# Hybrid attention and retention block: ScalarE issues the stores of its own results, retention is gated where it is computed, the states of both heads are built first, and the output projection takes its rows in order of readiness

## The chip, the cores and the metric

One core of one Trainium2 chip. Its engines run side by side, each through its own queue in order: TensorE (PE in the profile; PEld is its weight load), VectorE (DVE), ScalarE (ACT), GpSimd (POOL) and SyncE (SP, which computes nothing and issues transfers between HBM and the on-chip memory). The metric is the device time of one execution in microseconds; lower is better.

## What is computed

One encoder block on a sequence of 1024 tokens, model width 2048, all in float32. Cut to what matters:

```
h    = rmsnorm(x, norm_w)
q_a, k_a, v_a, g_a, q_r, k_r, v_r, g_r = split(h @ w_in)          # 2048 x 5632
attn = windowed_attention(q_a, k_a, v_a)    # 16 heads, 4 key/value heads, +-128 tokens
attn = rmsnorm(attn, w1) * silu(g_a)                              # width 1024
ret  = bidirectional_retention(rotary(q_r), rotary(k_r), v_r)     # 8 heads, chunks of 128
ret  = head_groupnorm(ret, w2) * silu(g_r)                        # width 1024
out  = rmsnorm(x + concat([attn, ret]) @ w_out, final_norm_w)     # 2048 x 2048
```

Retention runs over chunks in both directions: within a chunk it is a masked product, across chunks a state per head is carried, `state = state * decay + k^T v`.

## The kernel before

Each float32 operand of a large product is split into a high part (`wh`, `hT` part 0, rounded by ScalarE) and a low part (`wl`, the rest, by a subtraction on VectorE or GpSimd), and three matmuls (high x high, high x low, low x high) replace one. The program runs in four stretches:

- **The standard units** (`STD`, lines 1161 to 1163): keys, values and queries of the attention, 6 units.
- **The first half of the fast units** (`FAST`, 16 units of 256 columns: `ga` and `gr` are the gates, `qk` the retention's queries and keys, `vr` its values). A unit is a 2x2 block product done with 7 passes in place of 8, 12 matmuls each (`multiply`, lines 981 to 983), first over one half of the contraction, whose partial results go to HBM (`yd`), then over the other half. `prep` splits the weights of a pass two passes (slots) ahead, on ScalarE and GpSimd; `collect` adds a finished PSUM bank to the unit's result tile `e`, on VectorE. Attention (`attn_job`, 4 groups) is woven into this half.
- **The second half of the fast units**. A finished tile goes through `deliver`: gates through a SiLU on ScalarE and to HBM (`gd`, line 1059 and the store after it), values through a transpose on TensorE (`to_tokens`, lines 1086 and 1088), queries and keys through the rotary step (`rope`). Retention (`ret_job(p)`, 4 pairs p of 2 heads) is woven in here, and `premix`, which multiplies the attention's rows by their gates and norms on GpSimd.
- **The output projection** (lines 1295 to 1297, then 1321 to 1323): 16 rows k of `w_out` for each of 7 units `un`, 12 matmuls a row; `mixed_load` and `mixed_rows` bring the mixed activations of a row (`kk`, 0 to 7 attention, 8 to 15 retention) into `hT`.

What is woven in is cut into steps by `yield`. `point()` is called after every three matmuls, and every `pace` points it emits one step of `jobs` (attention, retention) and every `apace` points one of `aux` (premix and the like). So the text that a queue holds is written by the recording order; a scheduler that orders each engine's instructions then moves some past each other. `store()` does not issue at once: it keeps a store for some points (`delay`, 7 by default) and then gives it to SP. `lag(n, f)` runs `f` n slots later.

Of a pair p of retention the steps are: `k_tr` (transpose the keys), `s_t` (masked scores), `kv(ah, h)` (products of keys and values of head ah, sequence half h, and on VectorE the state tile `ST`, lines 707, 709 and 153), `o_mm` (output: lines 736 and 738, the second of which reads `ST`; statistics on VectorE), `o_fin`, `o_norm` (normalisation, line 766, ScalarE), `o_tr` (transpose, lines 773 and 776, store). One buffer `ST` serves both heads, so `kv(1, .)` stands after the outputs of head 0.

Buffers that matter: `t2` (6 tiles for everything in passing), `r` (9, weights of fast units), `e11`, `e12` (2 each), `e21`, `e22` (1 each, results of a unit and weights to come).

## Time and profile before

| | |
|---|---|
| time, 3 runs | 1571.16, 1574.75 (median), 1576.69 us |
| the profiled execution | 1579.63 us; its span in the trace 1577.9 us |
| TensorE, VectorE, ScalarE, GpSimd busy | 1485.4 (94%), 896.2, 675.1, 639.3 us |
| mean granted TensorE clock | 0.978 |
| HBM traffic | 216.38 MB read, 93.88 MB written |

The busy time of TensorE includes matmuls that wait in its pipeline and those that run at the lower clock, so the losses are read from its waits and from the granted clock, stretch by stretch. All 1145 transfers of the program are issued by SP.

### The profile page before, as it was taken

What the parts mean: (1) busy time and instruction counts of PE and PEld (TensorE: products, weight loads), DVE (VectorE), ACT (ScalarE), POOL (GpSimd) and SP (SyncE); (2) the same over time, 40 slices, a digit from 0 to 9 for tenths busy, and PEclk for the clock granted to TensorE, in tenths of its full rate; (3) what the DMA queues carried; (4) which work ended last, traced back from release to release, by engine and by line L of the source; (5) the groups of instructions that cost most, each with busy time, mean ns of one, the idle gap of its engine ahead of it and who ended that gap; (6) DMA issues with size and microseconds to landing.
All of it is one profiled execution on the core that took longest, in us unless ns stands there. A gap on an engine that the chain in (4) does not pass through costs nothing. (4 is left out here: it accounts for less than half of the span.)

```text
span 1577.9 us, 22010 instructions
## 1 busy us (share of the span) xinstructions
PE 1485.4 (94%) x7250; PEld 1233.9 (78%) x7250; DVE 896.2 (57%) x1856; ACT 675.1 (43%) x1417; POOL 639.3 (41%) x497
## 2 busy tenths in 40 slices
PE   8999999999999999999988988998879979999997
PEld 6898877878888888887867866777658767888886
DVE  6565346854664664668756767667485423364323
ACT  5311135865765775776322332433434423334210
POOL 3232221346556547555775565555641010113000
PEclk9999999999999999999999999999998999999999
DMA  8878768884454465538785675566855644566403
GB/s 302 290 263 304 265 177 266 263 251 156 154 159 146 149 182 174 153 112 289 240 281 182 194 235 176 189 181 196 269 170 160 235 146 158 156 215 207 125 27 107
DMA packets 195406, 311.73 MB, mean 198 GB/s; under 512 B 29355, under 2 KB 67243, under 8 KB 194652
## 3 DMA queue, kind: packets, MB, share of 16 engines
q1 hardware_dynamic: 195292, 310.33, 61.1%
q8 instruction: 57, 0.93, 0.3%
q14 instruction: 57, 0.47, 0.1%
HBM read 216.38 MB, written 93.88 MB: 197 GB/s over the span
## 5 line engine op out<-in xcount | busy, mean ns | idle before, releaser
L150 POOL TENSOR_TENSOR wl<-r,wh 128x512 fp32r<-128x512 f32 x224 | 302.4, 1356 | 287.9 <-ACT wh L156 278.3
L981 PE MATMUL psMa<-hT,wh 128*128 128x512 f32 x512 | 209.9, 410 | 4.4 <-DVE e L150 3.9
L156 ACT CAST wh<-r 128x512 fp32r<-128x512 f32 x224 | 137.5, 617 | 174.4 <-PE psMa L982 81.7
L983 PE MATMUL psMa<-hT,wl 128*128 128x512 f32 x512 | 203.5, 397 | 2.0 <-POOL wl L150 2.0
L982 PE MATMUL psMa<-hT,wh 128*128 128x512 f32 x512 | 203.0, 396 | 0.0
L156 ACT CAST wh<-e 128x512 fp32r<-128x512 f32 x160 | 97.6, 618 | 208.6 <-PE psMb L1297 74.3
L981 PE MATMUL psMb<-hT,wh 128*128 128x512 f32 x384 | 156.5, 408 | 4.3 <-DVE bnt L153 4.3
L983 PE MATMUL psMb<-hT,wl 128*128 128x512 f32 x384 | 152.9, 398 | 6.1 <-POOL wl L150 6.0
L150 DVE TENSOR_TENSOR wl<-e,wh 128x512 fp32r<-128x512 f32 x112 | 83.7, 757 | 131.8 <-ACT wh L156 126.8
L150 POOL TENSOR_TENSOR wl<-e,wh 128x512 fp32r<-128x512 f32 x48 | 71.8, 1499 | 205.0 <-ACT wh L156 197.7
L982 PE MATMUL psMb<-hT,wh 128*128 128x512 f32 x384 | 151.9, 396 | 0.0
L150 POOL TENSOR_TENSOR t<-t,t 128x512 f32<-128x512 f32 x48 | 64.5, 1345 | 134.1 <-DMA t<-gd 102.3
L983 PEld LDWEIGHTS psMa<-hT,wl 128*128 128x128 f32 x512 | 98.0, 191 | 25.6 <-POOL wl L150 3.7
L981 PEld LDWEIGHTS psMa<-hT,wh 128*128 128x128 f32 x512 | 98.4, 192 | 22.4 <-issue 4.7
L982 PEld LDWEIGHTS psMa<-hT,wh 128*128 128x128 f32 x512 | 98.5, 192 | 16.1
L590 DVE CUSTOM_DVE_ANT_0 P<-psST,bias,nsink 128x384 f32<-128x384 f32 (+1 forms) x128 | 74.3, 580 | 38.9 <-PE psST L582 37.9
L983 PEld LDWEIGHTS psMb<-hT,wl 128*128 128x128 f32 x384 | 73.2, 191 | 24.9 <-POOL wl L150 8.7
L150 DVE TENSOR_TENSOR r<-r,r 128x512 f32<-128x512 f32 x64 | 61.8, 977 | 51.2 <-POOL wl L150 50.8
L594 ACT ACTIVATE P<-P,nmx 128x385 f32<-128x385 f32 (+1 forms) x128 | 75.8, 592 | 30.8 <-DVE nmx L590 30.0
L981 PEld LDWEIGHTS psMb<-hT,wh 128*128 128x128 f32 x384 | 73.5, 191 | 17.7 <-issue 4.9
L150 POOL TENSOR_TENSOR r<-r,r 128x512 f32<-128x512 f32 x64 | 84.6, 1332 | 3.8
L982 PEld LDWEIGHTS psMb<-hT,wh 128*128 128x128 f32 x384 | 73.3, 191 | 12.4
(338 smaller groups left out, 3564.4 us busy)
## 6 DMA issues: line engine op xcount, KB each, us to landing
r<-in_w_fast SPq DMA_DIRECT2D x128, 256.0 KB, 3.4
e<-in_w_out SPq DMA_DIRECT2D x112, 256.0 KB, 3.3
yd<-e SPq DMA_DIRECT2D x64, 256.0 KB, 2.7
e<-yd SPq DMA_DIRECT2D x64, 256.0 KB, 3.2
t<-in_xT SPq DMA_DIRECT2D x31, 512.0 KB, 6.2
t<-cd SPq DMA_DIRECT2D x56, 256.0 KB, 4.0
e<-in_w_in SPq DMA_DIRECT2D x48, 256.0 KB, 5.0
md<-t SPq DMA_DIRECT2D x48, 256.0 KB, 3.1
```

Of the source, the lines that this page charges most:

```text
L150: eng.tensor_tensor(o, x, y, op)
L156: A.copy(o_hi, x)
L590: V.tensor_tensor_reduce(x[:, :W], p[:, :W], bias[2 * pr + c][:, k0 : k0 + W], -1.0, nsink[:, head : head + 1], ALU.add, ALU.min, nmx[:, c ...
L594: A.activation(x[:, : W + 1], x[:, : W + 1], AF.Exp, bias=nmx[:, c : c + 1], scale=-1.0, accum_out=sums[:, c : c + 1])
L981: T.matmul(bank, wh[:, ws], hh, start=(j == 0 and p in (0, 1, 3)), stop=False, skip_group_check=True)
L982: T.matmul(bank, wh[:, ws], hl, start=False, stop=False, skip_group_check=True)
L983: T.matmul(bank, wl[:, ws], hh, start=False, stop=(j == 3), skip_group_check=True)
```

## The change: what it does

1. `store_now`: the stores of `u` (attention outputs, 64), of the gates (32) and of `vr` (16) are issued by ScalarE right behind the operation that made them, not later by SP.
2. The order of the fast units: `gr` of a pair directly behind its `qk` and `vr`; the last two gates of the attention (`ga` 2 and 3) come last. `gate` runs 2 slots after the tile is done (before 1), `to_tokens` 3 (before 2).
3. `o_norm` loads the gate of its tile, and `o_tr` multiplies by it on VectorE while it reads the transposed result from PSUM (before: a copy on ScalarE, and the gate multiplied in later on GpSimd by `mixed_rows`).
4. Two state tiles, `ST0` and `ST1`: `kv` of both heads comes ahead of the first output; the buffer for this is that of one of the two `kT`. A pair has 34 steps for 31, at a pace of 2.42 points for 2.75.
5. Output rows are taken in the order `ROWS`, with the rows that are ready last at the end; `mixed_rows` works in three stages, one per call (wait, ScalarE, VectorE). `premix` is split by half, and half of it moves into the output projection.
6. Buffers: `e2` with 3 tiles in place of `e21` and `e22`, 8 `r` for 9; raw weights are loaded in another order; `pace` of the attention 2.65 for 2.7.

```diff
-FAST = [("ga", 0), ("qk", 0), ("vr", 0), ("qk", 1), ("vr", 1), ("ga", 1), ("qk", 2), ("vr", 2)]
-FAST += [("qk", 3), ("vr", 3), ("ga", 2), ("ga", 3)] + [("gr", _p) for _p in range(4)]
+FAST = [("ga", 0), ("qk", 0), ("vr", 0), ("gr", 0), ("qk", 1), ("vr", 1), ("gr", 1), ("ga", 1)]
+FAST += [("qk", 2), ("vr", 2), ("gr", 2), ("qk", 3), ("vr", 3), ("gr", 3), ("ga", 2), ("ga", 3)]
+ROWS = [0, 1, 2, 3, 8, 9, 10, 11, 12, 13, 4, 5, 14, 15, 6, 7]
...
+    def store_now(dst, src, then=None):
+        A.dma_start(dst, src)
+        if then is not None:
+            then()
...
-        return out_of(com, [128, 512], F32, tag, 2 if tag in ("e11", "e12") else 1)
+        return out_of(com, [128, 512], F32, tag, 3 if tag == "e2" else 2)
...
-                store(mpd[2 * g + pr, :, :, 128 * n : 128 * n + 128], u, u, last)
+                store_now(mpd[2 * g + pr, :, :, 128 * n : 128 * n + 128], u, last)
...
-            kT[h] = r4(f"kT{h}")
+            kT[h] = r4("kT")
...
-                ST[ah] = r4("ST")
+                ST[ah] = r4(f"ST{ah}")
...
+            e0 = RET + 128 * (2 * p + ah)
+            so = t2()
+            SP.dma_start(so, gd[e0 : e0 + 128, 512 * h : 512 * h + 512])
+            O[ah, h] = (on, so)
...
-            so = t2()
-            A.copy(so, q)
+            tt(V, so, q, so, ALU.mult)
...
+            ((kv, 0, 0),),
+            ((kv, 1, 0),),
             ((k_tr, 1),),
-            ((kv, 0, 0),),
             ((s_t, 0, 1),),
             ((kv, 0, 1),),
+            ((kv, 1, 1),),
             (),
             (),
             ((o_mm, 0, 0, 0),),
...
-        if kk >= 8:
-            g = t2()
-            SP.dma_start(g, gd[128 * kk : 128 * kk + 128, sl])
-        mixing.append([kk, hf, r, g])
+        if not mixed_ready(kk, hf):
+            drain(aux if kk < 8 else jobs, ("pre", kk, hf) if kk < 8 else ("ret", (kk - 8) // 2))
...
-                store(gd[128 * c : 128 * c + 128, sl], t, t, finished, 4)
-            lag(1, gate)
+                store_now(gd[128 * c : 128 * c + 128, sl], t, finished)
+            lag(2, gate)
...
-                store(dst, o.rearrange("p (c e) -> p c e", c=4), o, finished)
-            lag(2, to_tokens)
+                store_now(dst, o.rearrange("p (c e) -> p c e", c=4), finished)
+            lag(3, to_tokens)
...
-            pace[0], apace[0] = 2.75, 2.3
+            pace[0], apace[0] = 2.42, 2.2
...
-            if stage == 0:
-                drain(aux, ("pre", 7))
...
+            mixed_rows()
+            for kk in {0: (0, 1), 1: (2, 3), 3: (8, 9), 4: (10, 11), 5: (12,), 6: (13,)}.get(stage, ()):
                 mixed_load(kk, 0)
-                mixed_rows(2)
...
-                if un == 0 and k == 9:
-                    drain(jobs, ("ret", 3))
-                    mixed_load(14, 0)
-                    mixed_load(15, 0)
-                if un == 0 and k == 11:
-                    mixed_rows(0)
+                if un == 0:
+                    mixed_rows()
+                    if k in (5, 6, 7, 8, 9, 10):
+                        mixed_load(ROWS[k + 5], 0)
+                    if k == 13:
+                        mixed_flush()
```

What this does to the queues, first on VectorE where the state of the first pair is built. Before, for head 1 of the pair, behind the outputs of head 0 (names end in running numbers; `r` is a sum of weights, `bnt` a statistic, `e22` a tile of `collect`):

```order
L150 TENSOR_TENSOR r1951_9198<-r1920_9022,r1921_9023 128x512
L707 COPY ST1941_9125<-psST1940_9120 64x384
L153 SCALAR_TENSOR_TENSOR ST1941_9125<-ST1941_9125,cdec_97,psST1940_9120 64x128
L150 TENSOR_TENSOR bnt1950_9184<-bnv1934_9095,bny1935_9097 128x4
L150 TENSOR_TENSOR r1918_9020<-r1918_9020,r1920_9022 128x512
```

And in the change, for both heads ahead of the outputs (`ST0` is `ST01858`, `ST1` is `ST11866`):

```order
L717 COPY ST01858_8732<-psST1857_8727 64x384
L160 SCALAR_TENSOR_TENSOR ST01858_8732<-ST01858_8732,cdec_97,psST1857_8727 64x128 x4
L717 COPY ST11866_8769<-psST1865_8764 64x384
L160 SCALAR_TENSOR_TENSOR ST11866_8769<-ST11866_8769,cdec_97,psST1865_8764 64x128 x2
L157 TENSOR_TENSOR e12_1842_8664<-psMa1832_8627,e12_1842_8664 128x512
L160 SCALAR_TENSOR_TENSOR ST11866_8769<-ST11866_8769,cdec_97,psST1865_8764 64x128 x2
L157 TENSOR_TENSOR sd1872_8816<-psST1871_8811,dt1840_8652 128x512
L157 TENSOR_TENSOR e2_1852_8705<-psMa1799_8453,e2_1852_8705 128x512
L157 TENSOR_TENSOR r1860_8745<-r1860_8745,r1859_8744 128x512
L719 COPY ST01858_8732<-psST1876_8831 64x512
```

The work of head 1 has moved from between the two heads' outputs to directly behind that of head 0, and the chains of the two heads now share VectorE's queue. Next ScalarE in the attention: `u` is copied out of PSUM, and in the change its store follows (with what each waits for: `Activation` is ScalarE's own earlier result, `DMAHW` an earlier transfer). Before:

```order
L553 COPY u_1078_5323<-psO1077_5316 128x256 [waits DMAHW7_49,PE_49]
L571 CAST PTh1080_5329<-psST1079_5325 128x3x128 [waits PE_49]
L594 ACTIVATE P1085_5338,sums1084_5337<-P1085_5338,nmx1083_5336 128x385 [waits DVE_49]
L156 CAST wh1092_5387<-r980_4903 128x512 [waits PE_49,Pool_49]
L571 CAST PTh1080_5329<-psST1089_5363 128x3x128 [waits PE_49]
```

In the change:

```order
L563 COPY u_1082_5343<-psO1081_5336 128x256 [waits DMAHW7_49,PE_49]
L581 CAST PTh1084_5350<-psST1083_5346 128x3x128 [waits PE_49]
L107 DMA mpd_59<-u_1082_5343 256x1x128 [waits DMAHW5_49,Activation_49]
L163 CAST wh1091_5380<-r980_4904 128x512 [waits PE_49,Pool_49]
L604 ACTIVATE P1089_5359,sums1088_5358<-P1089_5359,nmx1087_5357 128x385 [waits DVE_49]
```

The store has come into ScalarE's queue one operation behind the copy, between two casts; it waits for the copy and for an earlier transfer. Last SP at the head of the output projection. Before, rows of retention with a gate each (lines 844 and 847), between stores of gates (line 98):

```order
L844 DMA t2_2480_11829<-md_58 128x512
L847 DMA t2_2481_11831<-gd_57 128x512
L844 DMA t2_2482_11836<-md_58 128x512
L847 DMA t2_2483_11838<-gd_57 128x512
L98 DMA md_58<-t2_2473_11781 128x512
L98 DMA gd_57<-e21_2448_11648 128x512
```

In the change:

```order
L780 DMA t2_2438_11690<-gd_57 128x512
L863 DMA t2_2440_11700<-md_58 128x512
L863 DMA t2_2441_11702<-md_58 128x512
L863 DMA t2_2450_11745<-md_58 128x512
L207 DMA e11_2486_11919<-in_w_out 128x512
L845 DMA t2_2457_11774<-md_58 128x512
L846 DMA t2_2458_11775<-gd_57 128x512
```

The rows come without a gate (line 863), the only gate there is that of `o_norm` (line 780), and the loads of `premix` (lines 845 and 846), which before were over by then, stand between the weights (line 207).

## Rows read from the trace of the kernel before

**Rows 1.** The page's first part: each engine's busy time, share of the span and instructions.

```profile
PE 1485.4 (94%) x7250; PEld 1233.9 (78%) x7250; DVE 896.2 (57%) x1856; ACT 675.1 (43%) x1417; POOL 639.3 (41%) x497
```

**Rows 2.** Busy time by stretch, in us: the attention's half, the retention's half, the start of the output projection, its rest. Columns: stretch, its length, PE, PEld, DVE, ACT, POOL, granted clock of TensorE (1 is the full one), share of the transfer engines, GB/s.

```profile
262.00:742.00 480.00, 470.58 (x2442) 399.91 (x2443) 295.56 (x755) 325.67 (x761) 258.33 (x196) 0.99 0.58 184
742.00:1222.00 480.00, 429.65 (x2100) 350.53 (x2099) 324.94 (x648) 167.30 (x317) 270.44 (x213) 0.95 0.65 208
1222.00:1350.00 128.00, 117.55 (x488) 93.32 (x487) 46.24 (x71) 41.92 (x80) 12.98 (x10) 0.96 0.54 175
1350.00:1577.90 227.90, 217.63 (x955) 178.52 (x953) 93.82 (x167) 62.25 (x125) 27.12 (x24) 0.99 0.44 141
```

**Rows 3.** What TensorE waited for in the retention's half (742 to 1222 us): us in total, times, longest.

```profile
PE psO L738 <- DVE ST L153: 26.2, 7, 7.1
PE psST L1086 <- DVE e L150: 6.3, 3, 2.9
PE psMb L983 <- POOL wl L150: 4.9, 4, 2.1
PE psMb L981 <- DVE bnt L153: 4.3, 1, 4.3
PE psMa L981 <- DVE e L150: 3.9, 2, 2.6
PE psMa L983 <- POOL wl L150: 2.0, 3, 0.9
```

**Rows 4.** The same at the start of the output projection (1222 to 1350 us).

```profile
PE psST L1295 <- ACT wh L156: 4.9, 3, 2.6
PE psMa L1295 <- ACT wh L156: 3.9, 2, 3.6
PE psST L1296 <- DVE wl L150: 1.0, 3, 0.4
```

**Rows 5.** Granted clock in two short stretches behind waits of TensorE (columns as in rows 2).

```profile
981.00:992.00 11.00, 6.49 (x22) 5.36 (x23) 7.34 (x20) 2.75 (x6) 1.59 (x2) 0.53 0.38 133
1182.00:1193.00 11.00, 9.21 (x29) 7.40 (x30) 10.55 (x21) 5.26 (x10) 3.48 (x3) 0.53 0.32 107
```

**Rows 6.** Two waits of line 981, the first matmul of a bank, in order of time (start, us, instruction, and in brackets the idle time before it).

```profile
981.18 0.66 PE L981 MATMUL psMa<-hT,wh 128*128 128x512 f32 x1 [1.38 <-DVE e L150]
...
1183.79 0.77 PE L981 MATMUL psMb<-hT,wh 128*128 128x512 f32 x1 [4.31 <-DVE bnt L153]
```

**Rows 7.** The seven waits of line 738 in order of time, written as in rows 6. They are pair 0 head 0, pair 0 head 1, and so on; the last is pair 3 head 0.

```profile
850.54 0.80 PE L738 MATMUL psO<-ST,qs 128*128 128x128 f32 x2 [5.98 <-DVE ST L153]
884.27 0.49 PE L738 MATMUL psO<-ST,qs 128*128 128x128 f32 x2 [1.04 <-DVE ST L153]
950.52 0.49 PE L738 MATMUL psO<-ST,qs 128*128 128x128 f32 x2 [1.74 <-DVE ST L153]
987.45 0.80 PE L738 MATMUL psO<-ST,qs 128*128 128x128 f32 x2 [4.33 <-DVE ST L153]
1049.44 0.49 PE L738 MATMUL psO<-ST,qs 128*128 128x128 f32 x2 [1.51 <-DVE ST L153]
1083.19 0.49 PE L738 MATMUL psO<-ST,qs 128*128 128x128 f32 x2 [4.55 <-DVE ST L153]
1151.26 0.80 PE L738 MATMUL psO<-ST,qs 128*128 128x128 f32 x2 [7.06 <-DVE ST L153]
```

**Rows 8.** VectorE at the last of these waits: the sum of weights ahead of the state chain, the chain's head, and its last piece.

```profile
1141.52 4.09 DVE L150 TENSOR_TENSOR r<-r,r 128x512 f32<-128x512 f32 x3 [6.95 <-POOL wl L150]
1145.64 0.69 DVE L709 COPY ST<-psST 64x512 f32<-64x512 f32 x1
...
1150.85 0.35 DVE L153 SCALAR_TENSOR_TENSOR ST<-ST,cdec 64x128 f32<-64x128 f32 x1
```

**Rows 9.** GpSimd shortly before: the multiplications of `premix` (`t<-t,t`), in pairs.

```profile
1126.04 2.66 POOL L150 TENSOR_TENSOR t<-t,t 128x512 f32<-128x512 f32 x2 [5.20 <-DMA t<-rbd]
...
1132.53 2.64 POOL L150 TENSOR_TENSOR t<-t,t 128x512 f32<-128x512 f32 x2 [2.59 <-DMA t<-rbd]
```

**Rows 10.** Groups of instructions by line: engine, operation, tiles, count, busy us, mean ns, idle before.

```profile
L862 ACT ACTIVATE hT<-t,ew 128x512 fp32r<-128x512 f32 x28 | 20.0, 720 | 41.7 <-POOL t L150 25.2 <-DMA t<-md 13.7 <-PE psMa L983 2.6
L150 POOL TENSOR_TENSOR t<-t,t 128x512 f32<-128x512 f32 x48 | 64.5, 1345 | 134.1 <-DMA t<-gd 102.3 <-DMA t<-rbd 28.7 <-DMA e<-yd 1.3
L150 DVE TENSOR_TENSOR e<-psMa,e 128x512 f32<-128x512 f32 x80 | 54.2, 682 | 29.4 <-PE psMa L983 26.7 <-ACT e L1018 1.7 <-issue 0.5
```

**Rows 11.** Transfers by kind: median us from issue to landing.

```profile
mpd<-u SPq DMA_DIRECT2D x64, 128.0 KB, 2.7
...
t<-gd SPq DMA_DIRECT2D x32, 256.0 KB, 4.5
```

**Rows 12.** One issue of a store on SP, in order of time (start, us it took).

```profile
1101.61 0.38 SPq L98 DMA_DIRECT2D md<-t  x1
```

**Rows 13.** What the stores of SP (line 98) waited for: us in total, times, longest.

```profile
SPq L98 <- ACT e L1059: 45.3, 20, 5.2
...
SPq L98 <- ACT u L553: 9.7, 3, 4.8
```

**Rows 14.** One matmul of 512 columns at the full clock, from the chain of work that ended last (start, us, what).

```profile
1319.23 0.23 PE psMa L1297
```

More of the change, by code (lines that the diff above doesn't have):

```diff
@@ L116, in et_ @@
     def et_(tag):
-        return out_of(com, [128, 512], F32, tag, 2 if tag in ("e11", "e12") else 1)
+        return out_of(com, [128, 512], F32, tag, 3 if tag == "e2" else 2)
     def rt(dt):
-        return wp.tile([128, 512], dt, tag="r", name=nm("r"), bufs=9)
+        return wp.tile([128, 512], dt, tag="r", name=nm("r"), bufs=8)
     def wpair(i):
@@ L191, in w_src @@
         if i >= W_STD:
-            return a["w_out"][(i - W_STD) % 64]
+            i -= W_STD
+            return a["w_out"][(ROWS[i] if i < 16 else i) % 64]
         u, j = divmod(i, 8)
@@ L519, in attn_job @@
         SP.dma_start(vs3[:, :, 64:128].bitcast(F32), vd[g])
-        yield
-        yield
+        for _ in range(4):
+            yield
+        vr3 = vs3[:, :, 64:128].bitcast(F32)
+        for hf in range(2):
+            sl = slice(512 * hf, 512 * hf + 512)
+            A.copy(kh[:, sl], kl[:, sl].bitcast(F32))
+        A.copy(vs3[:, :, 0:64], vr3)
         yield
@@ L823, in hybrid_block @@
     mixing = deque()
-    def premix(kk):
-        for hf in range(2):
-            sl = slice(512 * hf, 512 * hf + 512)
-            r, g, n = t2(), t2(), t2()
-            SP.dma_start(r, md[128 * kk : 128 * kk + 128, sl])
-            SP.dma_start(g, gd[128 * kk : 128 * kk + 128, sl])
-            SP.dma_start(n, rbd[:, sl])
-            for _ in range(3):
-                yield
-            tt(G, g, g, n, ALU.mult)
-            tt(G, r, r, g, ALU.mult)
-            yield
-            store(md[128 * kk : 128 * kk + 128, sl], r, r, (lambda: done.add(("pre", kk))) if hf else None)
-            yield
@@ L841, in mixed_load, with premix @@
-    def mixed_load(kk, hf):
-        r, g = t2(), None
-        sl = slice(512 * hf, 512 * hf + 512)
-        SP.dma_start(r, md[128 * kk : 128 * kk + 128, sl])
-        if kk >= 8:
-            g = t2()
-            SP.dma_start(g, gd[128 * kk : 128 * kk + 128, sl])
-        mixing.append([kk, hf, r, g])
-    def mixed_rows(keep):
-        for m in list(mixing)[: max(len(mixing) - 1, 0) if keep else None]:
-            if m[3] is not None:
-                tt(G, m[2], m[2], m[3], ALU.mult)
-                m[3] = None
-        while len(mixing) > keep:
+    def premix(kk, hf):
+        sl = slice(512 * hf, 512 * hf + 512)
+        r, g, n = t2(), t2(), t2()
+        SP.dma_start(r, md[128 * kk : 128 * kk + 128, sl])
+        SP.dma_start(g, gd[128 * kk : 128 * kk + 128, sl])
+        SP.dma_start(n, rbd[:, sl])
+        for _ in range(5):
+            yield
+        tt(G, g, g, n, ALU.mult)
+        tt(G, r, r, g, ALU.mult)
+        yield
+        store(md[128 * kk : 128 * kk + 128, sl], r, r, lambda: done.add(("pre", kk, hf)))
+        yield
@@ L857, in mixed_rows, with mixed_ready @@
+    def mixed_ready(kk, hf):
+        return ("pre", kk, hf) in done if kk < 8 else ("ret", (kk - 8) // 2) in done
+    def mixed_load(kk, hf):
+        if not mixed_ready(kk, hf):
+            drain(aux if kk < 8 else jobs, ("pre", kk, hf) if kk < 8 else ("ret", (kk - 8) // 2))
+        r = t2()
+        SP.dma_start(r, md[128 * kk : 128 * kk + 128, 512 * hf : 512 * hf + 512])
+        mixing.append([kk, hf, r, 0])
+    def mixed_rows():
+        while mixing and mixing[0][3] == 2:
             kk, hf, r, _ = mixing.popleft()
@@ L866, in evac, with mixed_flush @@
+    def mixed_flush():
+        while mixing:
+            mixed_rows()
     def evac(u, b, p, st):
@@ L940, in hybrid_block, with raw_room @@
     raws, sums, ready_w, banks, outs = {}, {}, {}, {}, {}
-    def raw_room(q):
+    def raw_room(q, which):
         if q < 2 * NF:
-            for x in (2, 1, 3, 0):
+            for x in which:
                 raws[q, x] = rt(F32)
@@ L1182, in hybrid_block @@
     step[0] = 16 * NS
[L1183 removed]
+    old, coming = deque(), deque()
     for n, (q, p) in enumerate(slots):
```

81 lines of the change are left out of this document (39 added, 42 removed).

## Prediction

> **What bounds the kernel now.** I read the busy shares first: TensorE is busy for 1485.4 of 1577.9 us, and no other engine for more than 57% [rows 1]. So the time is TensorE's work plus what it loses, and the other engines matter only where TensorE waits for them. The table by stretch [rows 2] shows where it loses. In the retention's half (742 to 1222 us) it is idle for 480 - 429.65 = 50 us and its clock stands at 0.95 on average; at the start of the output projection (1222 to 1350 us) it is idle for 10 us at 0.96. The attention's half loses 480 - 470.58 = 9 us and the rest of the projection about 10 us, most of it the program's end. The waits of TensorE then name the causes. In the retention's half it waits 26.2 us for the state tile `ST`, 6.3 us for result tiles to transpose, 8.2 us (4.3 + 3.9) for VectorE before it can start a bank, and 6.9 us (4.9 + 2.0) for GpSimd's low parts [rows 3]. These are 46.3 us (the idle time above also has gaps too short to be listed). In the projection it waits 9.8 us for split weights [rows 4].
>
> The clock costs as much again. Behind a long wait the granted clock is at its lower level: 981 to 992 us and 1182 to 1193 us show 0.53, which is almost all at 1.2 GHz in place of 2.4 [rows 5], and waits of 1.38, 4.33 and 4.31 us stand at their beginnings [rows 6, 7]. A stretch of length t at mean clock c loses about (1 - c) t: 0.05 x 480 = 24 us and 0.04 x 128 = 5 us, 29 us in all. Waits and clock together are 46.3 + 9.8 + 29 = 85 us in these two stretches. That is what this change can reach.
>
> **The change part by part.**
>
> *States of both heads early.* The seven waits for `ST` are of two kinds [rows 7]. Those of head 1 (1.04, 4.33 and 4.55 us) come because its state is only begun when head 0 is through, as the buffer is shared. With two tiles its chain is done thirteen steps before it is read; these 9.9 us go, and I see nothing that would bring them back. Those of head 0 (5.98, 1.74, 1.51 and 7.06 us, 16.3 in all) have another cause: VectorE comes to the chain late. For the last one, VectorE stood 6.95 us for GpSimd and then needed until 1151.2 us for the chain, from a head at 1145.6 [rows 8]; GpSimd was late because `premix` put pairs of 2.65 us into its queue while its operands were still landing [rows 9]. Half of `premix` leaves this stretch, but the chain gets longer: between its pieces the order now has pieces of head 1. From the matmuls of `kv(0, 1)` to the first output there are four steps of 2.42 points for three of 2.75, 9.7 points for 8.3, and the chain of 5.6 us [rows 8] takes on about 1 us of head 1's copy (0.69) and links (0.35 each). One cancels the other, so I keep half of the 16.3 and take 8 as gained.
>
> *Transposes of values and gates a slot later.* The tile is then finished when TensorE and ScalarE come to it. TensorE's 6.3 us for line 1086 [rows 3]: 5 gained.
>
> *Gate multiplied at the result, reordered gates, half of premix later.* In the second half this takes 8 of 16 `premix` halves (two multiplications of 1.345 us each, 21.5 us) and the gate multiplications of the mixed rows from GpSimd [rows 10]. VectorE gets 16 multiplications that read PSUM, at 0.682 us each 10.9 us (the nearest row is the accumulation of a bank, same shape, one operand in PSUM) [rows 10]; ScalarE loses 16 copies. Of the 15.1 us that TensorE waits for late VectorE and GpSimd (8.2 + 6.9) I take half, 7, as gained. Against it I set 5 us for VectorE: it is busy for 325 of 480 us there [rows 2], so about two thirds of 10.9 us can meet other work, and part of that reaches TensorE. Bounds: 0 and 10.9.
>
> *Rows in order of readiness.* Before, the rows of retention wait for GpSimd and for a gate that lands 4.5 us after its issue [rows 11], and ScalarE stands 25.2 us in its queue for that product, ahead of the weights' casts [rows 10]. Now the rows come ready, and three calls pass between load and use. Of 9.8 us I take 7 as gained. What is late next is `premix`, which now runs inside the projection; it has GpSimd almost to itself (busy 13 of 128 us) [rows 2].
>
> *Stores issued by ScalarE.* 112 issues leave SP. One takes 0.38 us there [rows 12]; the trace shows none on ScalarE, so that is my nearest row: 64 x 0.38 = 24 us in the attention's half, 18 us after it. ScalarE is idle for 480 - 326 = 154 us of the attention's half [rows 2], 2.4 us for each store, so most of it is covered: the casts behind a store prepare weights two slots ahead. I set 5 us; bounds 0 and 43. If the cover were gone, all that stands behind a store would be late by it: casts of weights and of attention probabilities, and then TensorE. SP is relieved of waiting as well: its stores stood 45.3 us for the SiLU and 9.7 us for `u` [rows 13], with loads queued behind. I give this no term of its own; it is part of why half of the late-engine waits go.
>
> The Trainium skill, page "DMA: Bandwidth & Descriptors", section "Issuing engines are not separate DMA queues", says that transfers run on the same 16 engines whoever issues them, and that another issuer saves only the time of issuing. No run here shows yet whether that holds; the rows above show the waiting of SP's queue beside its issuing. By the rule, half of the 7 us for late engines would be wrongly credited, and the sum 3 to 4 us higher.
>
> *Order of units, buffers, raw loads, pace.* The work of the units is the same. The weights' ring shrinks from 9 to 8 tiles and `raw 1` is loaded a slot later, while result tiles get one more. I set nothing for them; the two-slot lead of `prep` covers a load that is late by one slot, 12 matmuls of 0.23 us [rows 14] or 2.8 us, and beyond it every us is TensorE's.
>
> *The clock.* Gained waits are 9.9 + 8 + 5 + 7 + 7 = 36.9 of 56.1 us, two thirds. In proportion the clock would return 19 of 29 us. Short waits that stay can hold the lower level as well as long ones (1.38 us stood at the head of the first stretch of [rows 5]), so I take 13.
>
> *The sum.* -36.9 - 13 + 5 + 5 = -40 us. The profiled execution took 1579.6 us, so 1540 us; it stands 4.9 us (0.3%) above the median of 1574.75, so against the runs I forecast **1535 us**. Differences within 0.3%, about 4.7 us, can't be told from no change.
>
> **The rivals.**
>
> *All of it goes* (8%): no wait is left in both stretches, the clock returns, ScalarE and VectorE hide their share. 1575 - 85 = 1490 us, or 1500 with small costs. For it speaks that every named cause is touched; against it, that VectorE stays the busiest helper.
>
> *VectorE's burst* (15%): the chains of both heads stand back to back. One chain took 5.6 us with what stood between its pieces [rows 8]; two are 11 us, in a part of the pair of eight steps, 8 x 2.42 x 3 matmuls of 0.23 us or 13 us [rows 14], while masked scores and first chains have to be made and banks emptied too. Then TensorE waits at line 981 in place of 738. At 4 us for each of 4 pairs, with clock, 25 us come back: about 1560 us.
>
> *The gain is paid back* (8%): `o_tr` holds VectorE until its gate has landed. If loads are as late as GpSimd saw them (102.3 us of waiting [rows 10]) and each of 16 holds VectorE for 2 to 3 us, that is 40 us: 1575 us, no change. Against it: the load is three steps ahead, 3 x 2.42 x 3 x 0.23 = 5 us, against a landing of 4.5 us [rows 11].
>
> *ScalarE becomes the bound* (12%, slower): a store in its queue waits for its own copy and for an earlier transfer. As long as a store costs less than the 2.4 us of idle time that ScalarE has for each, TensorE doesn't see it. Above that, the attention's half grows by 64 times the rest. If a store stands for a transfer of 2.7 us [rows 11] and issues 0.4 us, 0.7 us each is over: 45 us, and with the lower clock behind such waits 60. Against 50 us of gain this ends at 1580 to 1590 us. For it speaks that ScalarE is the busiest helper there; against it, that the transfer it waits for is several issues old.
>
> **How the numbers follow.** My forecast has 57% and holds 1515 to 1558. With the best case (8%) and the burst (15%) faster by over 0.3% is 80%, no change 8%, slower 12%. For eight in ten the range has to reach half into the best case and over the case of no change: 1508 to 1576. The bounds of the unknown costs (VectorE 10.9, ScalarE 43) lie inside it, the second only with part of the gain.
>
> **What would show it.** Right: line 738 waits for `ST` under 10 us in all, none of them head 1's; line 1086 under 2 us; mean clock of the retention's half 0.97 or above, idle time there near 25 us; start of the projection near 3 us of waits. Wrong: stores of ScalarE followed by idle time over 2 us in the attention's half and TensorE's idle time there well above 9 us; VectorE waiting for the load of a gate in `o_tr`; waits at line 981 for VectorE above 8 us; waits of weights' casts for raw weights, which I priced at nothing.

## The result and the profile after

| | before | after |
|---|---|---|
| time, median | 1574.08 us (5 runs, 1571.16 to 1576.69) | 1581.75 us (5 runs, 1577.52 to 1585.18) |
| ratio, 95% interval | | 1.0048 [1.0026, 1.0071] |
| the profiled execution | 1579.63 us, span 1577.9 us | 1581.0 us, span 1579.2 us |
| mean granted clock | 0.978 | 0.980 |

The change makes the kernel 0.5% slower, 7.6 us. The forecast was 1535 us in a range of 1508 to 1576. The busy times of the changed kernel, then its table by stretch (columns as in [rows 2]):

```profile
PE 1486.1 (94%) x7250; PEld 1230.2 (78%) x7250; DVE 912.4 (58%) x1872; ACT 666.0 (42%) x1401; POOL 614.3 (39%) x481
```

```profile
262.00:742.00 480.00, 470.49 (x2442) 398.28 (x2443) 291.37 (x751) 324.69 (x756) 258.55 (x197) 1.00 0.60 183
742.00:1222.00 480.00, 426.09 (x2070) 342.23 (x2068) 336.20 (x658) 152.88 (x295) 246.74 (x197) 0.96 0.61 200
1222.00:1350.00 128.00, 123.39 (x516) 100.01 (x517) 52.52 (x76) 46.79 (x89) 11.13 (x8) 0.95 0.63 205
```

The work went where the diff sends it: GpSimd has 24 us less in the retention's half than in [rows 2], ScalarE 14 less, VectorE 11 more. But TensorE is idle there for 54 us where it was 50, and its clock is as low. A fixed stretch of time can't tell more, since the projection begins a little earlier in the change; so I also measure by the work. From the first matmul of the second half of the fast units to the first of the projection it is 465.6 us before and 464.8 after, from there to the end 380.8 and 384.2. What TensorE waits for has been exchanged. Its waits from 742 to 1222 us (us in total, times, longest):

```profile
PE psST L707 <- DMA vt<-vrd: 12.2, 4, 3.8
PE psMa L1003 <- POOL wl L157: 6.5, 9, 2.3
PE psMa L1001 <- DVE bmv L757: 6.5, 1, 6.5
PE psMa L1001 <- ACT wh L163: 4.8, 4, 2.8
PE psST L787 <- ACT on L776: 4.2, 3, 2.8
PE psMb L1001 <- DVE bmv L757: 3.8, 1, 3.8
PE psMa L1310 <- DVE wl L157: 3.5, 2, 3.3
PE psMb L1003 <- POOL wl L157: 2.7, 4, 1.4
PE psMa L1001 <- DVE e L157: 2.5, 2, 1.6
PE psO L748 <- DVE ST L160: 1.9, 2, 1.3
PE psMa L1309 <- ACT wh L163: 1.8, 1, 1.8
PE psMa L1309 <- DVE e L157: 1.2, 1, 1.2
PE psMa L1001 <- DVE bnt L157: 1.0, 1, 1.0
```

Lines have moved by 10 to 20: 748 is the old 738, 1001 to 1003 the old 981 to 983, 1309 and 1310 the old 1295 and 1296. Against [rows 3] the state tile fell from 26.2 to 1.9 us and the result tiles to transpose (6.3 us) are gone. In their place stand the load of the values, 12.2 us, VectorE ahead of a bank (line 1001), 13.8 us for 8.2, and ScalarE (`wh` at line 1001, `on`), 9.0 us for 1.9. The rows of lines 1309 and 1310 belong to the projection already.

The first newcomer is one pattern in all four pairs; this is the second pair: ScalarE's store of the last values, SP's load of the pair's values, TensorE's first product with them (start, us, what, in brackets the idle time before):

```profile
917.63 0.37 ACTq L107 DMA_DIRECT2D vrd<-t  x1
```

```profile
921.69 0.32 SPq L667 DMA_DIRECT2D vt<-vrd  x1
```

```profile
927.93 2.05 PE L707 MATMUL psST<-vt,kT 128*128 128x128 f32 x8 [3.22 <-DMA vt<-vrd]
```

`store_now` marks the values as ready when the store is recorded, and the new order of units lets the pair begin right then. Its load is issued 4 us after the store and needs another 6 (5.3 in the median of the four), and the product, now the third item in a pair's list of steps where it was the fourth, is there first.

The longest wait, 6.5 us, is a chain over three engines. TensorE wants a bank which VectorE's sum at 1005.70 empties; VectorE had stood 7.93 us for a tile of the ring `t2` that GpSimd's `premix` still used (the rotary step writes into it); GpSimd had stood for a transfer (the trace names a load of partial results):

```profile
1000.85 2.60 POOL L157 TENSOR_TENSOR t<-t,t 128x512 f32<-128x512 f32 x2 [3.46 <-DMA e<-yd]
```

```profile
1003.50 0.01 DVE L1090 LOAD_MASK_SELECT t<-e  x1 [7.93 <-POOL t L157]
...
1005.70 0.65 DVE L157 TENSOR_TENSOR e<-psMa,e 128x512 f32<-128x512 f32 x1
```

```profile
1006.50 0.77 PE L1001 MATMUL psMa<-hT,wh 128*128 128x512 f32 x1 [6.49 <-DVE bmv L757]
```

At the start of the projection the waits at its two lines (1309, 1310) are 7.9 us for 9.8 in [rows 4], but another 3 us at these lines now fall ahead of 1222 us (the wait of 3.3 us lies across 1222 us and stands in both lists). Its waits from 1222 to 1350 us:

```profile
PE psMa L1310 <- DVE wl L157: 3.3, 1, 3.3
PE psST L1309 <- ACT wh L163: 2.6, 2, 1.9
PE psST L1310 <- DVE wl L157: 2.0, 3, 1.4
```

### The profile page after: what moved, and what is told of

The parts are those of the page before. It is cut to its first block, busy times and chain, and to the rows that moved or that the text cites. A ratio compares the mean times of both kernels' runs of the same rounds, so it can differ in the third digit from the quotient of the medians.

```text
span 1579.2 us, 21950 instructions
## 1 busy us (share of the span) xinstructions
PE 1486.1 (94%) x7250; PEld 1230.2 (78%) x7250; DVE 912.4 (58%) x1872; ACT 666.0 (42%) x1401; POOL 614.3 (39%) x481
## 4 chain that ended last, share of the span: by engine, by line
PE 50%; DMA 17%; DVE 10%; issue 9%; POOL 7%; ACT 4%; SPq 3%; POOLq 0%; ACTq 0%; DVEq 0%
POOL wl L157 4%; PE psMa L1003 4%; PE psMa L1001 4%; PE psMa L1002 4%; PE psMb L1001 3%; PE psMb L1003 3%; PE psMb L1002 3%; PE psST L574 2%; DMA t<-mpd 2%; PE psST L1310 2%; PE psMa L1310 2%; PE psST L1309 2%; DMA cd<-crow 2%; PE psST L1311 2%; DVE t L157 2%
## 5 line engine op out<-in xcount | busy, mean ns | idle before, releaser
L157 DVE TENSOR_TENSOR wl<-e,wh 128x512 fp32r<-128x512 f32 x112 | 85.6, 770 | 137.0 <-ACT wh L163 134.7
L1003 PEld LDWEIGHTS psMb<-hT,wl 128*128 128x128 f32 x384 | 72.9, 190 | 22.7 <-POOL wl L157 6.5
L157 DVE TENSOR_TENSOR r<-r,r 128x512 f32<-128x512 f32 x64 | 60.1, 952 | 35.7 <-POOL wl L157 34.1
L157 POOL TENSOR_TENSOR hT<-t,hT 128x512 fp32r<-128x512 f32 x16 | 21.4, 1335 | 130.7 <-ACT hT L163 130.7
```

The lines of the kernel that those rows point to most:

```text
L157: eng.tensor_tensor(o, x, y, op)
L1003: T.matmul(bank, wl[:, ws], hh, start=False, stop=(j == 3), skip_group_check=True)
```

## The experiments

Each kernel was timed in five rounds beside the kernel before; gains and losses below are the ratios times 1575 us, against the kernel before unless another is named. Executions of one kernel lie up to 14 us apart, and a profile shows one of them, so differences under some 5 us between single traces are not read as gains. "Base" stands for the changed kernel with the stores of gates and values given back to SP (experiment f1), from which later edits start.

| kernel | median us | ratio, 95% interval |
|---|---|---|
| e1 states of both heads alone, on before | 1569.0 | 0.9960 [0.9944, 0.9976] |
| e2 stores by ScalarE alone, on before | 1584.7 | 1.0073 [1.0049, 1.0098] |
| e3 change, all stores by SP | 1567.6 | 0.9952 [0.9934, 0.9971] |
| e4 change, pair begun 2 slots later | 1574.0 | 0.9994 [0.9976, 1.0011] |
| f1 change, only `u` by ScalarE (base) | 1567.6 | 0.9960 [0.9942, 0.9977] |
| f2 change, only gates and values by ScalarE | 1582.7 | 1.0062 [1.0041, 1.0083] |
| f3 change, stores at the same places by SP | 1584.9 | 1.0058 [1.0034, 1.0083] |
| f4 base, gates by ScalarE at once | 1580.2 | 1.0048 [1.0029, 1.0067] |
| g1 f4, gates marked ready 2 slots later | 1574.9 | 0.9997 [0.9979, 1.0016] |
| g2 base, gates by ScalarE 4 points later | 1575.3 | 1.0002 [0.9984, 1.0020] |
| g3 base, pair begun 1 slot later | 1569.7 | 0.9963 [0.9948, 0.9978] |
| g4 base, no multiplications in `premix` | 1543.4 | 0.9814 [0.9787, 0.9840] |
| h1 base, half of `premix` kept back | 1563.3 | 0.9922 [0.9901, 0.9942] |
| h2 base, `o_norm` 1 step later | 1571.6 | 0.9978 [0.9966, 0.9990] |
| h3 base, `o_norm` 2 steps later | 1561.2 | 0.9914 [0.9897, 0.9930] |
| h4 base, SiLU of gates 1 slot later | 1563.3 | 0.9935 [0.9921, 0.9949] |
| k1 h1, h3 and h4 together | 1557.3 | 0.9893 [0.9870, 0.9916] |
| k2 f4, no multiplications in `premix` | 1551.8 | 0.9854 [0.9827, 0.9881] |

**Parts alone and taken back.** e1 puts part 4 on the kernel before (step list and pace of the change):

```
-            kT[h] = r4(f"kT{h}")
+            kT[h] = r4("kT")
-                ST[ah] = r4("ST")
+                ST[ah] = r4(f"ST{ah}")
```

> The kernel before with part 4 of the change alone: two state tiles, one tile for transposed keys, the 34 steps of a pair at a pace of 2.42. Theory of the prediction: the waits for ST fall from 26.2 to under 9 us and nothing of that size takes their place; with the clock about 25 us are gained, 1550 us. Rival (VectorE's burst, in the prediction): the waits move to the first matmul of a bank, behind VectorE; 1568 to 1580 us. Rival (the values' load, seen in the changed kernel): the first product of keys and values is now a step nearer to the load of the values, and TensorE waits there 1 to 4 us in each pair; 1565 us.

It gains 6 us, where the prediction had 18 for the waits alone. Its waits in the retention's half (lines as in the kernel before, but behind the list of steps moved by 3: 984 to 986 are 981 to 983, 1089 is 1086):

```profile
PE psST L1089 <- DVE e L150: 13.8, 7, 4.3
PE psMb L986 <- POOL wl L150: 7.9, 7, 4.3
PE psMb L984 <- DVE e L150: 6.0, 1, 6.0
...
PE psST L697 <- DMA vt<-vrd: 2.5, 1, 2.5
...
PE psO L738 <- DVE ST L153: 1.8, 2, 1.2
```

The waits for `ST` fell by 24 us, but all waits of this half together, measured by the work, only from 49.6 to 45.9: those at other lines rose, 13.8 for 6.3 us at the transposes, 10.3 for 6.9 at the low parts, and smaller ones. Is that the rival of VectorE's burst? Of the seven waits at line 1089 one (3.1 us, at 943 us) has a state chain ahead of it on VectorE. The longest has none (TensorE's wait, then what VectorE did before it):

```profile
987.15 0.87 PE L1089 MATMUL psST<-ident,e 128*128 128x128 f32 x4 [4.34 <-DVE e L150]
```

```profile
981.35 0.69 DVE L150 TENSOR_TENSOR r<-r,r 128x512 f32<-128x512 f32 x1 [2.44 <-POOL wl L150]
981.96 1.77 DVE L150 TENSOR_TENSOR e<-e,t 128x512 f32<-128x512 f32 x1
983.77 1.64 DVE L150 TENSOR_TENSOR qs<-rq,qd 64x512 f32<-64x512 f32 x1
```

VectorE stood for GpSimd, and then came a sum of weights, the rotary step, the scaled queries and statistics. So the burst has the smaller part in these waits; mostly VectorE is late with its ordinary work.

e2 puts part 1 on the kernel before, e3 takes it out of the changed kernel:

```
-                store_now(gd[128 * c : 128 * c + 128, sl], t, finished)
+                store(gd[128 * c : 128 * c + 128, sl], t, t, finished, 4)
```

> The kernel before with part 1 of the change alone: ScalarE issues the 112 stores. Theory: the attention's half hides them as it does in the changed kernel (its idle time of TensorE stays within 2 us of 9.4), time within 5 us of the kernel before. Prediction: 5 us slower, bounds 0 and 43. Rival: ScalarE's stores are what costs, 10 us or more slower, to be seen as waits for casts (wh, PTh).

> The changed kernel without part 1: SP issues all stores again, some points later, as before. Theory: the values count as ready only when the later store is given out, so a pair begins later, and TensorE's 12.2 us of waiting for the values' load fall under 4; 1581 - 10 = 1571 us or better. Rival (it is the issuing engine that matters): ScalarE loses 30 to 40 us of issues and SP's loads stand behind stores again; weights come late, 1585 us or more. Rival (neither matters): 1581 us within 3.

Both say the same: part 1 costs 11.5 us on the kernel before and 15 us in the change. Without it the change gains 7.6 us. The theory of e2 fails with that, that of e3 comes out, the wait for the values' load included: it is not among the waits of e3.

e4 lets a pair begin later:

```
-                store_now(dst, o.rearrange("p (c e) -> p c e", c=4), finished)
+                store_now(dst, o.rearrange("p (c e) -> p c e", c=4), lambda: lag(2, finished))
```

> The changed kernel, with one edit: the values count as ready two slots after the last of their stores, so that a pair's loads and steps begin two slots later. Theory (values' load): the 12.2 us of TensorE's waits for vt at line 707 go, and with them a part of the lower clock behind them, 5 us; 1581 - 17 = 1564 us. Rival (the waits only move: VectorE is the one that is late, whatever TensorE does before): 12 us appear at other lines, 1578 to 1584 us.

The waits for `vt` are gone from its trace, and it gains 8.5 us against the change; but 9.0 us now stand at one place in front of the projection (line 1309), 18 us at line 1003. g3 makes the same edit (one slot) on the base:

> The changed kernel with stores of gates and values on SP, and a pair begun one slot later than its values' last store. Theory 1 (each wait counts by itself): the 5.2 us of waits for vt go, with the clock 7 us: 1560 us. Theory 2 (TensorE's waits in the retention's half are kept up by a loop of the helper engines; what one line loses another gains): listed waits stay at 77 to 86 us in all, 1565 to 1571 us.

There the waits for `vt` fall from 5.2 to 1.6 us, and the time stays. Both numbers of theory 2 come out, 77.4 us of waits and 1569.7 us; that a loop of helpers keeps them up is its explanation, not shown by this run.

**Which stores, and what about them.** f1 gives gates and values back to SP (the `store` lines of the kernel before), f2 `u`, f4 the values. f3 leaves the places and changes the issuer:

```
     def store_now(dst, src, then=None):
-        A.dma_start(dst, src)
+        SP.dma_start(dst, src)
```

> The changed kernel, but SP issues the stores of gates and values again; ScalarE keeps the 64 stores of u. Theory (the attention's half hides the stores of u): same time as with all stores on SP, 1566 to 1570 us. Rival (what the prediction feared: ScalarE's time in the attention's half): 1578 to 1584 us.

> The changed kernel, but SP issues the 64 stores of u again; ScalarE keeps those of gates and values. Theory (what the stores cost, they cost in the retention's half): 1578 to 1584 us, as the changed kernel. Rival (the stores of u are the cost): 1566 to 1570 us.

> The changed kernel with its stores recorded at the same places, but issued by SP in place of ScalarE. Theory 1 (it is the early place that costs: values count as ready at once, a pair's loads stand right behind): 1578 to 1584 us with TensorE's waits for vt still there. Theory 2 (it is the issuing engine: the loads of SP are tied to stores that another queue gives out): 1566 to 1572 us. Rival: SP stands for each result in front of its loads, over 1590 us.

> The changed kernel, but SP issues the 16 stores of the values again, some points later; ScalarE keeps those of u and of the gates. Theory 1 (the values' stores cost, since the pair begins right behind them): 1566 to 1572 us, no waits for vt over 1 us. Theory 2 (the gates' stores cost: result tiles come free only when a store of another queue has landed, and SP's loads into them stand for it, 65 us in the changed kernel): 1576 to 1582 us.

The 64 stores of `u` by ScalarE cost nothing that can be measured: f1 and e3 agree. The gates' stores alone make the difference: f4 is 14 us above f1, f2 without the early stores of `u` is as slow as the change, and the values' stores add nothing to f4's. Theory 1 of f4, that it is the values, falls; nor does their wait go with the stores given back to SP (f4):

```profile
PE psST L707 <- DMA vt<-vrd: 4.8, 2, 3.7
```

This sits badly with e4, which marks the values about as late as f4 does (two slots, eight points, for seven points), keeps their early store, and is 8.5 us faster than the change. So the 8.5 us of e4 can't be put down to the mark of the values; what else they are is open.

At the early place it matters little for the total who issues: f3 is as slow as the change. Part of that is chance. With `u` stored early by SP, the second half of the fast units begins at 739.4 us in f3 and at 730.2 in the change; the retention's half behind it is equally long, 467.3 us in f3, 466.5 in f4, 464.8 in the change, 456.0 in f1.

g1 keeps ScalarE's early store and marks the gate as ready later (`lambda: lag(2, finished)`); g2 lets ScalarE store at the place where SP does:

> The changed kernel, values stored by SP again, gates by ScalarE at once, but counted as ready only two slots later (their readers, premix above all, start later). Theory 1 (the early mark costs, since readers' loads stand in SP's queue right behind a store that has not landed): 1566 to 1572 us. Theory 2 (the early store itself costs, by what the order of SP's loads makes of it): 1577 to 1583 us, as without the later mark.

> The changed kernel, values stored by SP again, gates stored by ScalarE but four points after their result, where SP stored them. Theory (the place costs, whoever issues): 1566 to 1572 us. Rival (a second issuing queue for the gates costs at any place): 1577 to 1583 us.

Neither theory holds, in either run. The later mark takes back 8 of the 14 us; storing and marking four points later takes back 7; SP in place of ScalarE at that later place takes back the rest. SP's loads do stand longer for gates that another queue stores (its waits at line 1027, where a result tile must be free: change, then f1),

```profile
SPq L1027 <- DMA gd<-e: 65.5, 16, 8.8
```

```profile
SPq L1027 <- DMA gd<-e: 23.0, 10, 5.1
```

and this wait goes with the times of the kernels in which ScalarE stores the gates (g1 42.3 us, g2 43.9, f4 48.4), but it alone doesn't order all of them: f3 shows 28.2 us there and is as slow as the change.

**The helpers.** g4 takes GpSimd's part of `premix` out of the base (`G.memset` of one column in place of each multiplication, so that tiles, loads and stores stay):

> The changed kernel with stores of gates and values on SP, without the two multiplications of premix on GpSimd (its loads and stores stay; the attention's rows reach the projection without norm and gate). Theory (GpSimd's queue, in which the low parts of weights stand behind premix, is what TensorE meets last: 16.4 us of waits at line 1003): these waits halve, 1557 to 1562 us. Rival (GpSimd only follows ScalarE's casts, which follow TensorE): 1565 to 1570 us.

This is the largest effect of all, 23 us against the base. Table by stretch of f1, then of g4, from 742 us on:

```profile
742.00:1222.00 480.00, 427.75 (x2102) 344.85 (x2101) 344.07 (x664) 154.85 (x303) 250.48 (x199) 0.97 0.63 204
1222.00:1350.00 128.00, 123.16 (x524) 99.62 (x524) 53.22 (x76) 46.79 (x88) 12.56 (x9) 0.98 0.64 210
```

```profile
742.00:1222.00 480.00, 442.66 (x2188) 358.57 (x2187) 337.69 (x673) 160.51 (x311) 219.71 (x204) 0.98 0.67 218
1222.00:1350.00 128.00, 128.00 (x566) 106.02 (x566) 52.83 (x75) 49.50 (x93) 6.66 (x7) 1.00 0.59 189
```

GpSimd is busy for half of that stretch, and yet 31 us less of its work return half as much to TensorE; in the projection's first part, 1222 to 1350 us, TensorE no longer waits at all. Whether it is GpSimd's time, the `t2` tiles that `premix` holds meanwhile (the chain of 6.5 us above), or VectorE's work that GpSimd makes longer (last section; VectorE is busy for 6 us less in g4) these runs don't separate. k2 makes the same edit on f4:

> The changed kernel with the values stored by SP and the gates by ScalarE at once, without the two multiplications of premix on GpSimd (its loads and stores stay; the attention's rows reach the projection without norm and gate). With gates stored by SP this left 1543 us. Theory (the early stores of gates cost through the helpers' queues, which run short of GpSimd's time): with that time given back their 12 us shrink to 5 or less, 1543 to 1548 us. Rival (they cost by transfers or by SP's order, whatever GpSimd does): 1553 to 1557 us.

The early stores still cost 6 us there in place of 14, between theory and rival; the two intervals overlap a little, so the 6 us are uncertain by as much. That about half of their cost passes through the same shortage would fit, but is not shown.

h1 keeps `premix` of all second halves back until the second column block of the projection, and loads the retention's rows first there:

```
-                for hf in range(2):
-                    for kk in half:
-                        aux.append((after(premix(kk, hf), ("ga", kk // 2)), None))
+                for kk in half:
+                    aux.append((after(premix(kk, 0), ("ga", kk // 2)), None))
+            for kk in range(8):
+                aux.append((after(premix(kk, 1), "late"), None))
```

> The changed kernel with stores of gates and values on SP; premix of all second halves is kept back until the second column block of the output projection, and the second halves of the retention's rows are loaded first there. It leaves 4 halves of premix fewer in the retention's half and 4 fewer at the start of the projection. Theory (a half of premix costs there what leaving out the multiplications showed, 31 us for 16 halves, about 2 us each): 1567.6 - 8 x 2 = 1552 us. Rival (what those 8 halves cost was not GpSimd's time but their place beside the last rows; they now stand beside the weights' splits of the second block): 1562 to 1570 us.

It gains 6 us against the base, where the rate of g4 promised 16: the range of the rival. Its reason, the place beside other work, was not looked into. h2 and h3 move `o_norm` (and `o_tr`) by one and two steps, h4 writes `lag(3, gate)`. The first of the four places in h3:

```
-            ((o_norm, 0, 0), (o_mm, 0, 1, 0)),
+            ((o_mm, 0, 1, 0),),
             ((o_mm, 0, 1, 1),),
-            ((q_dec, 1, 0), (s_t, 1, 1)),
+            ((o_norm, 0, 0), (q_dec, 1, 0), (s_t, 1, 1)),
```

> The changed kernel with stores of gates and values on SP; the normalisation of a retention result (line 776, ScalarE) comes one step later in each of the four places of a pair. Theory (ScalarE stands 111 us there for VectorE's statistics, and the weights' casts behind it, GpSimd's low parts and in the end TensorE stand with it): these 111 us fall to about 70, TensorE's waits at line 1003 shrink; 1556 to 1562 us. Rival (ScalarE's standing hurts nobody, since the casts behind it wait for TensorE anyway): 1565 to 1570 us.

> As the one before, but two steps later. Theory: ScalarE's standing falls to about 40 us, 1552 to 1560 us. Rival: 1565 to 1570 us.

> The changed kernel with stores of gates and values on SP; the SiLU of a gate comes three slots behind its tile in place of two. Theory (ScalarE stands 79 us at the SiLU for VectorE's sum, with casts behind it): these fall by a third or more, 1560 to 1564 us. Rival (no one behind it is held up): 1565 to 1570 us.

h3 gains 7 us against the base; h4 gains 4 and h2 loses 3, with intervals that overlap the base's. But not for the reason given: ScalarE's standing at line 776 did not shrink in h3 (f1, then h3; the kernel before had 53.8 us there),

```profile
ACT on L776 <- DVE bnt L160: 111.4, 16, 12.4
```

```profile
ACT on L776 <- DVE bnt L160: 105.3, 15, 11.9
```

since the normalisations stand where they were in ScalarE's queue, though they are recorded later: in both traces the four of the first pair begin at its 962nd, 972nd, 982nd and 991st instruction (issues not counted), and those of the other pairs differ by two places at most. So the theory of ScalarE's standing was not tested. What moved is the order of other queues: 341 of TensorE's 7250 instructions stand elsewhere than in f1, and 141 of VectorE's 1872; in h2 96 and 20. Which of these moves gains, and why h3 is faster than h2, stays open. In h4 ScalarE's standing at the SiLU is 74.0 us for 78.6 in f1, not a third less, so its time lies in the theory's range without the theory's reason.

> The changed kernel with stores of gates and values on SP, with three of the edits tried singly: premix of second halves kept back, normalisation two steps later, SiLU of gates a slot later. If their gains (4, 6 and 4 us) add up: 1553 us. If what one edit removes comes back at another line, as so often here: 1560 us, no better than the best single one.

k1 is the fastest complete kernel, 16.9 us (1.1%) below the kernel before and 24 below the change. Its retention half:

```profile
742.00:1222.00 480.00, 442.28 (x2178) 358.41 (x2177) 339.70 (x670) 159.23 (x308) 239.10 (x191) 0.98 0.63 203
```

TensorE is busy for 16 us more of it than in the change. The three edits gained 17 us singly and 10.6 together, between the two forecasts: part of what each removes comes back.

## Why the prediction was wrong

**The step that failed** is the credit for removed waits: "Gained waits are 9.9 + 8 + 5 + 7 + 7 = 36.9 of 56.1 us". It took each wait as a sum of its own, and the clock's 13 us went by the same credit. With the 5 us for stores left out, the sum was -45 us; without the stores by ScalarE (e3) the change gains 7.6. These 37 us are mainly the error of this step (5 us for VectorE are in the sum too); the stores, priced at 5 us and measured at 15, make the other 10. Added up from the matmul records (all waits over 0.25 us of an execution, the program's start and end too), TensorE waits 79.8 us before and 80.4 after, and between 76.1 and 85.6 us in all of e1 to e4, f1 to f4 and g1 to g3, whatever lines they show (h2 79.7). It waits clearly less where helpers' work was left out, g4 60.0 and k2 63.7; kept back or recorded in another order it gives 72.9 (h1), 74.3 (h4), 70.3 (h3) and 65.0 (k1). My reading of that: a wait of TensorE in this half is the place where it meets helpers that feed each other, ScalarE's cast, GpSimd's low part, VectorE's sum over the same tile, and letting TensorE run past one of them brings it sooner to the next. e1 shows it for the waits for `ST`; for the other terms it is argued from the sums.

The sum of waits is not the whole time, though. f4 is slower than f1 by 14 us, and their traces differ in the retention's half by 10.5 us (466.5 and 456.0), while their waits there are 48.2 and 46.8 us. Most of the rest is the clock: by the prediction's (1 - c) t, an estimate, it loses 22.2 us there in f4 and 11.9 in f1. The granted clock of the whole execution was 0.979 to 0.982 in all five executions of the change and 0.983 to 0.990 in the twelve of f1. In the traces of the change and of f1 a like sum is cut into pieces of another size: from 262 us to the program's end phase, waits over 2 us make 34.0 us in the change and 24.7 in f1, and the clock stands there at the lower of its two levels (1.2 and 2.4 GHz) for 58.0 and 34.1 us. That the size of the pieces is the cause was not tested.

Term by term:
- *States* (18 us): as waits at line 738 more than right, 24 us gone, and both waits left at line 748 in the change are head 0's; as time 6 us in e1, clock included. "I see nothing that would bring them back" overlooked that VectorE and GpSimd are late for what TensorE wants next.
- *to_tokens* (5): gone, as forecast, but no time could be seen from it.
- *Late VectorE and GpSimd* (7): wrong sign. 15.1 us became 23.0 (13.8 at line 1001, 9.2 at line 1003), and 9.0 us for ScalarE joined them.
- *Start of the projection* (7): nothing. From the first matmul of the projection to that of its fourth column block the matmul records give 151.5 us before, 153.1 after, 153.9 in f1, 140.1 in g4, and TensorE's waits in it 9.9, 10.9, 11.6 and 1.3 us. "It has GpSimd almost to itself" led astray: GpSimd is idle for most of that time, and yet without the multiplications of `premix` (g4) the waits are gone. By which way `premix` reaches TensorE there is open; the waits named are for ScalarE's casts and VectorE's low parts of the weights.
- *Clock* (13): 0.978 became 0.980, which is 3 us. It was taken in proportion to the waits, which does not hold: with nearly the same sum of waits (81.9 and 80.4 us) f1 has 0.987 and the change 0.980, 11 us by (1 - c) t. The sum of [rows 3] was also added up wrongly, 46.3 us for 47.6, so that "36.9 of 56.1" should read 57.4; this moves the term by less than 1 us.
- *VectorE* (5 of 10.9): it is busy 11 us more, as counted; the rival that expected it at line 981 named the line of the 6.5 us. Its price, 25 us in a gain of 40, left 15 us of gain that is not there.
- *ScalarE's stores* (5, bounds 0 and 43): the size lay within the bounds, the place did not. An issue took 0.52 us for `u`, 0.34 for a gate, 0.38 for values:

```profile
L107 ACTq DMA_DIRECT2D mpd<-u x64: 520/521/602, 267.8 to 713.0; - x64
L107 ACTq DMA_DIRECT2D gd<-e x32: 326/338/390, 737.3 to 1199.1; - x32
L107 ACTq DMA_DIRECT2D vrd<-t x16: 366/377/399, 786.2 to 1130.8; - x16
```

  Together 50 us, but the 33 us in the attention's half are covered, as I argued: the first matmul of the second half of the fast units starts at 731.5 us before and 730.2 us after (84 matmul records a unit, counted). The rival "ScalarE becomes the bound" got the sign of the whole, and with 1580 to 1590 us even the time, but by luck: it spoke of the 64 stores of `u`, which cost nothing, and the 14 us come with 32 gates in the retention's half, of which no step of the prediction spoke.
- *Not in the sum*: the early mark. `finished` runs when a store is recorded, so readers' loads and steps stand right behind a store that has not landed. That makes the wait for `vt`, and marking the gates later (g1) gives back 8 us of their 14; for the values no price can be named, since e4 and f4 disagree. The diff showed it (`then()` in `store_now`, against `pend` in `store`); I read it as an edit of the issuing engine alone.

The Trainium skill, page "DMA: Bandwidth & Descriptors", section "Issuing engines are not separate DMA queues", says that another issuer saves only the time of issuing. f1 and e3 (0.9960 and 0.9952) agree with it for `u`: taking 64 issues off SP gained nothing that can be measured. For the gates another issuer at the same place cost 7 us (g2 against f1).

Of the signs that I set up, line 748 under 10 us and the transposes under 2 came true; clock above 0.97, idle time near 25 us and 3 us of waits in the projection did not. Of those for "wrong", waits for VectorE above 8 us at the first matmul of a bank came true; in the change's trace VectorE never waits for the load of a gate, so the gain was not paid back in `o_tr`, and among the named waits for casts of weights in the retention's half none is for a load of raw weights.

**Open**: by which way early stores of gates cost their last 6 to 7 us with ScalarE as issuer, what e4 gains, and what h3 does that h2 does not. One rival stands against all effects of 4 to 8 us (e4, g1, g2, h1, h3, h4, k2): each edit also reorders the queues, as h3 shows, and no run changes the order alone to show what that is worth. The effects of 14 us and more (gates at the early place, `premix`) are shown by two kernels each at least: f1 and e3 against f4 and the change, g4 and k2 against f1 and f4.

## What to carry to other kernels

Before crediting a removed wait, ask who is late next: add up the waits of the bound engine over the stretch, and expect much of that sum to stay unless work leaves the engines that feed it. Look at the granted clock beside it, since two kernels with the same sum can differ there. Taking 31 us off a helper that was busy for half of the time was worth more than removing 24 us of the longest waits. When a store moves, look at who is told that it is done and when, not only at who issues it.

## What the runs showed of the hardware

VectorE's work gets longer while GpSimd works, if both its inputs lie in SBUF. Two forms of a link of the state chain in the changed kernel, both 64x128, min/median/max in ns; the first reads PSUM, the second only SBUF:

```profile
L160 DVE SCALAR_TENSOR_TENSOR ST<-ST,cdec,psST x56: 327/339/342, 835.6 to 1159.8; 64x128 f32<-64x128 f32 x56
L160 DVE SCALAR_TENSOR_TENSOR ST<-ST,cdec x48: 346/352/1474, 848.3 to 1166.0; 64x128 f32<-64x128 f32 x48
```

The 26 SBUF links beside which no tensor operation of GpSimd ran took 0.351 us on average, the 22 others 0.916; the PSUM form took 0.337 either way. The sums of weights (`r<-r,r`) took 0.68 us alone (33 of them) and 1.24 on average beside GpSimd (31), and 0.69 and 1.23 in the kernel before. I had priced a link at 0.35, and GpSimd's work as if only its own queue paid for it. The Trainium skill, page "SBUF — State Buffer", section "SBUF: two separate sides", says that the two engines share a pair of ports, and that whichever starts first keeps it for the whole instruction, VectorE's operations with two SBUF inputs included where the GpSimd operation reads SBUF; these rows agree.
